# Moving the first weight operands of two stages into the stage ahead, and a token scale behind a DRAM round trip

## The chip, the cores and the metric

The kernel runs on one core of a Trainium2 chip. The metric is device time in microseconds of one execution. Before the change three executions took 1373.17, 1372.91 and 1370.94 us, median 1372.91. Five engines matter here: TensorE (PE, with its weight loads as PEld), VectorE (DVE), ScalarE (ACT), GpSimd (POOL) and SyncE (SP). The last two issue most of the DMAs.

## The reference

One decoder layer on 1024 tokens of width 1024, float32:

```python
h = rmsnorm(x, ln_mix); z = h @ w_in          # q, k, v, g, pool channels pu, gate logits
ret = retention_chunkwise(rotary(q), rotary(k), v)          # 4 heads, chunks of 128
y_ret = (silu(g) * groupnorm(ret) * gn_gain) @ w_ret_up
y_pool = multiscale_pool(pu, pool_w, pool_scale) @ w_pool_up   # windows 2, 4, 8, 16
mixed = sigmoid(gate_A) * y_ret + sigmoid(gate_B) * y_pool
x = x + mixed @ w_o
x = x + relu(rmsnorm(x) @ w_up) ** 2 @ w_down
out = rmsnorm(x, ln_final)
```

The pooling is linear in its input: moving sums over 2, 4, 8 or 16 tokens, divided by the count, minus the token itself.

## The kernel before

**Numbers.** Each float32 operand is carried as a pair: a rounded high part (ScalarE, line 134 or 94) and the remainder (VectorE, line 135 or 95). A product is three matmuls (high by high, high by low, low by high), `PASSES`. RMSNorm's gain goes into the operand, and the token's scale (`R1` for the first norm, `R2` for the second) is multiplied onto the product when it leaves PSUM.

**Stages.** Projection of q, k, v with the retention of four heads (`rotary`, `values`, `retain`, `transposed`); pooling input (`pool_input`, lines 497 to 505), interleaved with `mixed_blocks`; twelve mixer units for g and the gate logits (`mixer_unit`, lines 535 to 590); retention up-projection with the pooling (`pool`, lines 598 to 620); pooling up-projection; output projection (lines 691 to 718); sixteen up units (`up`, lines 721 to 749); the down projection as four sweeps; the final norm.

**The seven-product units.** Mixer and up units (`seven`, lines 180 to 245) multiply a 2 by 2 arrangement of blocks with seven block products in place of eight, in the form with shared sums (T1 to T4 on the token side, s1 to s4 on the weight side). A unit loads 1 MB of weights (line 182), forms s3, s1, s2 and s4 on VectorE (line 192), splits seven stationary operands (lines 134 and 135), and multiplies each with four moving blocks, 12 matmuls of 128x512 for each product, into PSUM banks X, Y, Z and V. The moving blocks of T1 to T4 are sums over tokens' halves: `mixed_blocks(k)` makes block k for the mixer (load from DRAM at line 509, scale at 512, sums at 520, splits), and `moving_operands` (lines 672 to 689) makes block k for up.

**First units.** With `late` (mixer 0 and up 0), the unit first does three quarters of four products:

```python
        if late:
            rest = (3,)
            for x, (ps, made) in groups.items():
                stationary(x, *made)
                mult(ps, x, range(3))
```

so the fourth moving block may come last. All of it stands in program order behind the whole stage ahead: for mixer 0 behind `mixed_blocks(3)` and the transposes of head 3's result (`transposed`, lines 463 to 473); for up 0 behind the copies of R2 (line 718), whose sums need the last residual add (line 706).

**Order of the work.** The engines' instruction streams are not in the order of the text: the tile framework schedules them at build time over a simulated time line, earlier text first where two instructions are ready. Each engine then runs its own stream in order. Buffers rotate: four of tag `w` (8 KB in each partition: weight pieces, raw unit weights, units' temporaries, `xw` blocks), nine of tag `a` (stationary operands of the units, `u`, `rn`, `retn`, `m`, `x1`, `R1`, `R2`), sixteen each of `h` and `r`, five PSUM banks `mm` and three `aux`. A tile waits until the tile that held its buffer is done with.

**Around the change.** `pool_input(g)` multiplies 48 times 128x512, and VectorE takes each half out of PSUM times R1 (line 504) into `u`, which goes to DRAM (line 505). `pool(g)` reads it back some 250 us later (line 601). In the output projection's last block row (k = 3) the order is tile 3 then tile 7 for the first half of the tokens, then both for the second.

Of the kernel before, what the change touches and what calls it, by code (L numbers as in the profile page):

```python
# [16 lines left out]
P = 128  # L17
# [21 lines left out]
def block_kernel(ctx: ExitStack, tc: tile.TileContext, a: dict, out: bass.AP):  # L39
# [33 lines left out]
    def pair_tile(tag, name):  # L73
        return a_tile(tag, name, F32R, (P, 2, HALF))
# [7 lines left out]
    def w_tile(name, dtype=F32R):  # L82
        return wpool.tile([P, 2 * S], dtype, tag="w", name=name)
# [93 lines left out]

    B11, B21, B22, T1, T2, T3, T4 = range(7)

    def seven(name, src, moving, done, late=False, after=None):  # L180
        raw = w_tile(f"raw_{name}", F32)
        nc.sync.dma_start(raw, src)
        raw = raw.rearrange("p (b j) -> p b j", b=4)
        a11, a12, a22, a21 = (raw[:, i, :] for i in range(4))
        tmp = w_tile(f"tmp_{name}", F32).rearrange("p (b j) -> p b j", b=4)
        p1, u2, u4, s3 = (tmp[:, i, :] for i in range(4))
        s1, s2, s4 = a21, a11, a12
        ws = {}

        def stationary(x, src, *adds):  # L190
            for dst, u, v in adds:
                nc.vector.tensor_tensor(dst, u, v, ALU.add)  # L192
            ws[x] = pair_tile("a", f"w{x}_{name}")
            split_pair(ws[x], src)

        def mult(ps, x, ks=range(4), start=True):
            for k in ks:
                for n, (sa, sb) in enumerate(PASSES):
                    nc.tensor.matmul(  # L199
                        ps, ws[x][:, sa, k * P : (k + 1) * P], moving[x][k][:, sb, :],  # L200
                        start=start and k == 0 and n == 0, stop=k == 3 and n == 2,
                        skip_group_check=not start,
                    )

        X, Y = mm_bank(f"ps_X{name}"), aux_bank(f"ps_Y{name}")
        Z, V = mm_bank(f"ps_Z{name}"), mm_bank(f"ps_V{name}")
        groups = {
            B11: (X, (a11,)),
            T2: (Y, (s2, (s3, a11, a21), (s1, a21, a22), (s2, s1, a11))),
            T1: (Z, (s1,)),  # L210
            T3: (V, (s3,)),
        }
        rest = range(4)
        if late:
            rest = (3,)
            for x, (ps, made) in groups.items():
                stationary(x, *made)
                mult(ps, x, range(3))

        def opening(x):  # L220
            ps, made = groups[x]
            if not late:
                stationary(x, *made)
            mult(ps, x, rest)

        def closing(ps, x, *made):
            stationary(x, *made)
            mult(ps, x, start=False)

        opening(B11)  # L230
        nc.scalar.activation(p1, X, AF.Copy)
        opening(T2)
        nc.vector.tensor_tensor(u2, p1, Y, ALU.subtract)
        closing(X, B21, a12)
        done(0, 0, X)
        if after:
            after()
        opening(T1)
        nc.vector.tensor_tensor(u4, u2, Z, ALU.add)
        opening(T3)  # L240
        done(1, 1, V, u4)
        closing(Z, B22, s4, (s4, a12, s2))
        done(0, 1, Z, u2)
        closing(V, T4, a22)
        done(1, 0, V, u2)

    def token_blocks(lo, hi):
# [249 lines left out]
    def pool_input(g):  # L497
        w = load_piece(a["w_fm"][8 + g], f"w_pu{g}")
        u = a_tile("a", f"u{g}")
        for half in range(2):  # L500
            sl = slice(half * HALF, (half + 1) * HALF)
            ps = mm_bank(f"ps_pu{g}_{half}")
            feature_major(ps, w, hT, half)
            nc.vector.tensor_tensor(u[:, sl], ps, R1[:, sl], ALU.mult)
        nc.gpsimd.dma_start(u_dram[g], u)

    def mixed_blocks(k):
# [17 lines left out]
    for g in range(1, 4):  # L525
        pool_input(g)
        mixed_blocks(g - 1)
    mixed_blocks(3)
    transposed(NH - 1, rn)

# [1 line left out]
    ret_dram = dram_tile("ret_dram", (KT // 2, P, 2, S))  # L532
    sg_dram = dram_tile("sg_dram", (2 * KT, P, S))

    def mixer_unit(i, late=False, after=None):
        swish = i < 4
        f0 = i if swish else (i - 4) // 4 * KT + i % 4
        tiles = (f0, f0 + 4)
        o = [a_tile("h", f"mx{i}_{f}") for f in tiles]
        if swish:  # L540
            for m, f in enumerate(tiles):
                nc.gpsimd.dma_start(o[m], retn_dram[f])
        left = [2, 2]

        def done(m, half, ps, add=None):
            sl = slice(half * HALF, (half + 1) * HALF)
            dst, f = o[m][:, sl], tiles[m]
            sign = -1.0 if m else 1.0
            if swish:
                t = rpool.tile([P, 2, HALF], F32, tag="raw", name=f"sw{f}_{half}")  # L550
                z, sig = t[:, 0, :], t[:, 1, :]
            else:
                z = ps if add is None else dst
            y = ps
            if add is not None:
                nc.vector.tensor_tensor(z, add, ps, ALU.add)
                y = z
            if swish:
                nc.vector.scalar_tensor_tensor(z, y, sign, R1[:, sl], ALU.mult, ALU.mult)
                nc.scalar.activation(sig, z, AF.Sigmoid)  # L560
                nc.vector.scalar_tensor_tensor(
                    dst, dst, vec[:, V_GNG + f : V_GNG + f + 1], sig, ALU.mult, ALU.mult
                )
                nc.vector.tensor_tensor(dst, dst, z, ALU.mult)
            else:
                nc.vector.tensor_tensor(z, y, R1[:, sl], ALU.mult)
                nc.scalar.activation(
                    dst, z, AF.Sigmoid, scale=sign, bias=vec[:, V_BG + f : V_BG + f + 1]
                )
            left[m] -= 1  # L570
            if not left[m]:
                nc.gpsimd.dma_start(ret_dram[f // 2, :, f % 2, :] if swish else sg_dram[f], o[m])

        seven(f"mx{i}", a["w_mix"][i], hx, done, late=late, after=after)

    retT = []

# [9 lines left out]
                    retT[-1].append(dst)  # L587

    for i in range(12):
        mixer_unit(i, late=i == 0, after=load_ret if i == 11 else None)  # L590


    pw_raw, pw = a_tile("r", "pw_raw", shape=(P, HALF)), pair_tile("r", "pw")
# [4 lines left out]
    def pool(g):  # L598
        win = WINDOWS[g]
        u = a_tile("r", f"uf{g}")  # L600
        nc.sync.dma_start(u, u_dram[g])
        cur = u
        step = 1
        while step < win:
            nx = a_tile("r", f"s{g}_{step}")
            nc.vector.tensor_copy(nx[:, :step], cur[:, :step])
            nc.vector.tensor_tensor(nx[:, step:], cur[:, step:], cur[:, : S - step], ALU.add)
            cur = nx
            step *= 2
        nc.vector.tensor_tensor(cur[:, :16], cur[:, :16], corr[:, g, :], ALU.mult)  # L610
        nc.vector.scalar_tensor_tensor(cur, cur, 1.0 / win, u, ALU.mult, ALU.subtract)
        ypT.append([])
        for half in range(2):
            pooled = pair_tile("r", f"pooled{g}_{half}")
            split_pair(pooled, cur[:, half * HALF : (half + 1) * HALF])
            ps = aux_bank(f"ps_pw{g}_{half}")
            exact(ps, lambda s: pw[:, s, g * P : (g + 1) * P], lambda s: pooled[:, s, :])
            dst = pair_tile("h", f"ypT{g}_{half}")
            split_scaled(dst, ps, vec[:, V_PSC + g : V_PSC + g + 1])
            ypT[g].append(dst)  # L620
# [70 lines left out]
    for k in range(4):  # L691
# [2 lines left out]
        if k == 3:  # L694
            order = [(f, half) for half in range(2) for f in (k, k + 4)]
        ws = {}
        for f, half in order:
            if f not in ws:
                x1[f] = a_tile("a", f"x1_{f}")
                nc.gpsimd.dma_start(x1[f], a["xT"][f * P : (f + 1) * P, :])  # L700
                ws[f] = load_piece(a["w_o"][f], f"w_o{f}")
                gained[f] = a_tile("r", f"gained{f}")
            sl = slice(half * HALF, (half + 1) * HALF)
            ps = mm_bank(f"ps_o{f}_{half}")
            feature_major(ps, ws[f], mixT, half)
            nc.vector.tensor_tensor(x1[f][:, sl], x1[f][:, sl], ps, ALU.add)
            add_squares(sums2[:, half, :], x1[f][:, sl], f == 0, f"{f}_{half}")
            nc.scalar.activation(
                gained[f][:, sl], x1[f][:, sl], AF.Copy,
                scale=vec[:, V_LNL + f : V_LNL + f + 1],  # L710
            )
# [1 line left out]
            nc.gpsimd.dma_start(x1_dram[f], x1[f])  # L713
        moving_operands(h2, k, gained[k], gained[k + 4], "r" if k < 2 else "h")
    R2 = a_tile("a", "R2")
    for half in range(2):
        sl = slice(half * HALF, (half + 1) * HALF)
        nc.vector.tensor_copy(R2[:, sl], token_rstd([sums2[:, half, :]], f"b{half}"))


    def up(j):
# [8 lines left out]
        def done(m, half, ps, add=None):  # L730
# [13 lines left out]
                nc.gpsimd.dma_start(act_dram[3][j], t4)  # L744

        seven(
            f"up{j}", a["w_up"][j], h2, done, late=j == 0,
            after=begin_down if j == NJ - 1 else None,
        )


# [329 lines left out]
```

## Time and profile before

| | us |
|---|---|
| median of three executions | 1372.91 |
| lowest, highest | 1370.94, 1373.17 |
| profiled execution, its own time | 1370.83 |
| its span, first to last instruction | 1369.0 |
| TensorE busy (6572 matmuls) | 1353.6 |
| VectorE busy | 987.9 |
| ScalarE busy | 565.1 |
| GpSimd busy | 86.1 |
| mean granted TensorE clock | 0.997 |

Times in rows are microseconds from the span's start. A row of a timeline gives start, duration, engine, line, operation, what it writes and reads, and a count where like instructions follow each other; in brackets stands the idle time of that engine just before, and what ended it. Matmuls overlap, so the duration of a row of matmuls ends later than the next row starts. A row of the windows gives the stretch and its length, each engine's busy time in it with the count of instructions, then the granted TensorE clock as a share of 2.4 GHz, the busy share of the DMA engines, and GB/s.

### The profile page before, as it was taken

What the parts mean: (1) busy time and instruction counts of PE and PEld (TensorE: products, weight loads), DVE (VectorE), ACT (ScalarE), POOL (GpSimd) and SP (SyncE); (2) the same over time, 40 slices, a digit from 0 to 9 for tenths busy, and PEclk for the clock granted to TensorE, in tenths of its full rate; (3) what the DMA queues carried; (4) which work ended last, traced back from release to release, by engine and by line L of the source; (5) the groups of instructions that cost most, each with busy time, mean ns of one, the idle gap of its engine ahead of it and who ended that gap; (6) DMA issues with size and microseconds to landing.
All of it is one profiled execution on the core that took longest, in us unless ns stands there. A gap on an engine that the chain in (4) does not pass through costs nothing. (4 is left out here: it accounts for less than half of the span.)

```text
span 1369.0 us, 17491 instructions
## 1 busy us (share of the span) xinstructions
PE 1353.6 (99%) x6572; PEld 1138.6 (83%) x6572; DVE 987.9 (72%) x1631; ACT 565.1 (41%) x960; POOL 86.1 (6%) x151
## 2 busy tenths in 40 slices
PE   9999999999999999999999999999999999999997
PEld 6998999878888888888887888888888888888886
DVE  5766565789966768628657878777787977689665
ACT  6234425463334344113445433333333544444372
POOL 0000001111000000000001011101111000000000
PEclk9999999999999999999999999999999999999999
DMA  9122021354342367124422344433437989778423
GB/s 360 50 62 77 17 92 63 124 215 158 121 172 85 112 238 261 62 77 170 154 77 77 116 169 169 151 126 147 169 139 292 407 330 351 261 266 307 159 70 123
DMA packets 65444, 225.07 MB, mean 164 GB/s; under 512 B 7376, under 2 KB 9424, under 8 KB 61264
## 3 DMA queue, kind: packets, MB, share of 16 engines
q1 hardware_dynamic: 47152, 158.66, 32.7%
q0 software_dynamic: 17920, 65.02, 12.5%
q8 instruction: 51, 0.84, 0.3%
q10 hardware_dynamic: 288, 0.29, 0.1%
q14 instruction: 33, 0.27, 0.1%
HBM read 167.31 MB, written 56.62 MB: 164 GB/s over the span
## 5 line engine op out<-in xcount | busy, mean ns | idle before, releaser
L121 PE MATMUL ps_v<-w_v_hi,hT 128*128 128x256 f32 x512 | 96.0, 284 | 0.0
L199 PE MATMUL ps_Xup<-mv,w_up 128*128 128x512 f32 x384 | 93.0, 390 | 1.7 <-DVE w_up L135 1.7
L199 PE MATMUL ps_Zup<-mv,w_up 128*128 128x512 f32 x384 | 92.5, 389 | 0.8 <-ACT w_up L134 0.8
L853 PE MATMUL ps_dnX<-db,da 128*128 128x512 f32 x384 | 93.1, 389 | 0.1
L134 ACT ACTIVATE w_up<-raw_up 128x512 fp32r<-128x512 f32 x96 | 58.3, 627 | 84.4 <-DVE raw_up L192 46.3
L199 PE MATMUL ps_Vup<-mv,w_up 128*128 128x512 f32 x384 | 92.6, 389 | 0.0
L121 PE MATMUL ps_yr<-retT,w_ret 128*128 128x512 f32 x384 | 88.5, 389 | 0.5 <-ACT w_ret L94 0.5
L121 PE MATMUL ps_o<-mixT,w_o 128*128 128x512 f32 x384 | 87.5, 389 | 0.0
L199 PEld LDWEIGHTS ps_Xup<-mv,w_up 128*128 128x128 f32 x384 | 71.9, 188 | 16.9 <-DVE w_up L135 2.1
L121 PEld LDWEIGHTS ps_yr<-retT,w_ret 128*128 128x128 f32 x384 | 72.0, 188 | 15.8 <-ACT w_ret L94 0.9
L199 PEld LDWEIGHTS ps_Zup<-mv,w_up 128*128 128x128 f32 x384 | 72.0, 188 | 15.7 <-ACT w_up L134 0.8
L853 PEld LDWEIGHTS ps_dnX<-db,da 128*128 128x128 f32 x384 | 72.0, 188 | 15.5 <-DVE db L135 0.5
L199 PEld LDWEIGHTS ps_Vup<-mv,w_up 128*128 128x128 f32 x384 | 72.0, 188 | 15.1 <-ACT w_up L134 0.2
L121 PEld LDWEIGHTS ps_o<-mixT,w_o 128*128 128x128 f32 x384 | 72.0, 188 | 15.0
L135 DVE TENSOR_TENSOR w_up<-raw_up,w_up 128x512 fp32r<-128x512 f32 x96 | 64.2, 685 | 26.4 <-ACT w_up L134 26.1
L121 PEld LDWEIGHTS ps_v<-w_v_hi,hT 128*128 128x128 f32 x512 | 80.8, 192 | 0.0
L134 ACT ACTIVATE w_mx<-raw_mx 128x512 fp32r<-128x512 f32 x72 | 43.6, 626 | 86.0 <-DVE raw_mx L192 44.0
L121 PE MATMUL ps_v<-w_v_lo,hT 128*128 128x256 f32 x256 | 72.6, 284 | 0.0
L199 PE MATMUL ps_Xmx<-hT,w_mx 128*128 128x512 f32 x288 | 72.0, 396 | 0.3 <-ACT w_mx L134 0.3
L199 PE MATMUL ps_Vmx<-hx,w_mx 128*128 128x512 f32 x288 | 69.5, 389 | 0.0
L728 ACT ACTIVATE act<-act 128x512 f32<-128x512 f32 x64 | 40.3, 629 | 65.6 <-DVE act L727 62.2
L199 PEld LDWEIGHTS ps_Xmx<-hT,w_mx 128*128 128x128 f32 x288 | 55.1, 192 | 12.5 <-ACT w_mx L134 0.6
(249 smaller groups left out, 2819.9 us busy)
## 6 DMA issues: line engine op xcount, KB each, us to landing
act_dram<-act POOLq DMA_DIRECT2D x48, 512.0 KB, 4.7
ad<-act_dram SPq DMA_DIRECT2D x48, 512.0 KB, 6.6
raw_up<-in_w_up_dram SPq DMA_DIRECT2D x16, 1024.0 KB, 5.0
raw_mx<-in_w_mix_dram SPq DMA_DIRECT2D x12, 1024.0 KB, 6.2
sg_dram<-mx POOLq DMA_DIRECT2D x16, 512.0 KB, 4.7
wa_lo<-in_w_down_dram SPq DMA_DIRECT2D x16, 512.0 KB, 9.0
wb_hi<-in_w_down_dram SPq DMA_DIRECT2D x16, 512.0 KB, 7.5
wc_lo<-in_w_down_dram SPq DMA_DIRECT2D x16, 512.0 KB, 4.3
```

What stands on the lines that cost most here:

```text
L121: nc.tensor.matmul(ps, stationary(k, sa), moving(k, sb), start=i == 0, stop=i == n - 1)
L134: nc.scalar.activation(dst[:, 0, :], src, AF.Copy)
L135: nc.vector.tensor_tensor(dst[:, 1, :], src, dst[:, 0, :].bitcast(F32), ALU.subtract)
L199: nc.tensor.matmul(ps, ws[x][:, sa, k * P : (k + 1) * P], moving[x][k][:, sb, :], start=start and k == 0 and n == 0, stop=k == 3 and n == ...
L728: nc.scalar.activation(dst, dst, AF.Square)
L853: nc.tensor.matmul(banks[i][:, c0 : c0 + n], w[:, sa, i * P : (i + 1) * P], x[:, sb, c0 : c0 + n], start=start and j == 0 and m == 0, stop ...
```

## The change

Three edits. The unit becomes an object: its load, buffers and stationary operands can be begun before its products. Mixer 0's unit is created, and its B11 operand made, ahead of `mixed_blocks(3)`; up 0's unit is created, and B11, T2, T1 and T3 made, ahead of tile 7's first half in the output projection. The token scales R2 move behind up 0's four three-quarter groups. And `pool_input` leaves PSUM by a ScalarE copy without R1, which `pool` multiplies onto the tile that it has read back.

```diff
-    def seven(name, src, moving, done, late=False, after=None):
+    class Unit:
+        def __init__(self, name, src):
+            self.name, self.ws = name, {}
+            raw = w_tile(f"raw_{name}", F32)
+            nc.sync.dma_start(raw, src)
...
+            self.made = {
+                B11: (a11,),
+                T2: (s2, (s3, a11, a21), (s1, a21, a22), (s2, s1, a11)),
+                T1: (s1,), T3: (s3,), B21: (a12,), B22: (s4, (s4, a12, s2)), T4: (a22,),
+            }
+        def stationary(self, x):
+            if x not in self.ws:
+                src, *adds = self.made[x]
+                for dst, u, v in adds:
+                    nc.vector.tensor_tensor(dst, u, v, ALU.add)
+                self.ws[x] = pair_tile("a", f"w{x}_{self.name}")
+                split_pair(self.ws[x], src)
+            return self.ws[x]
+        def begin(self, *xs):
+            for x in xs:
+                self.stationary(x)
+            return self
+    def seven(unit, moving, done, late=False, opened=None, after=None):
...
         if late:
             rest = (3,)
-            for x, (ps, made) in groups.items():
-                stationary(x, *made)
+            for x, ps in groups.items():
                 mult(ps, x, range(3))
+        if opened:
+            opened()
...
@@ pool_input
-            nc.vector.tensor_tensor(u[:, sl], ps, R1[:, sl], ALU.mult)
+            nc.scalar.activation(u[:, sl], ps, AF.Copy)
@@ after pool_input(3) and mixed_blocks(2)
+    first_mx = Unit("mx0", a["w_mix"][0]).begin(B11)
     mixed_blocks(3)
     transposed(NH - 1, rn)
@@ pool
         nc.sync.dma_start(u, u_dram[g])
+        nc.vector.tensor_tensor(u, u, R1, ALU.mult)
@@ output projection
-        for f, half in order:
+        for n, (f, half) in enumerate(order):
+            if k == 3 and n == 1:
+                first_up = Unit("up0", a["w_up"][0]).begin(B11, T2, T1, T3)
@@ token scales, now called by up 0's unit as `opened`
-    for half in range(2):
-        sl = slice(half * HALF, (half + 1) * HALF)
-        nc.vector.tensor_copy(R2[:, sl], token_rstd([sums2[:, half, :]], f"b{half}"))
+    def token_scales():
+        for half in range(2):
+            sl = slice(half * HALF, (half + 1) * HALF)
+            nc.vector.tensor_copy(R2[:, sl], token_rstd([sums2[:, half, :]], f"b{half}"))
```

## Rows read from the trace of the kernel before

**Rows 1.** The page, busy time of the engines and its share of the span.

```profile
PE 1353.6 (99%) x6572; PEld 1138.6 (83%) x6572; DVE 987.9 (72%) x1631; ACT 565.1 (41%) x960; POOL 86.1 (6%) x151
```

**Rows 2.** The chain of work that ended last, up stage: start, us, what.

```profile
816.28 2.72 PE ps_Xup L199 x12
```

**Rows 3.** Windows: stretch, length, PE, PEld, DVE, ACT, POOL busy, clock, DMA, GB/s.

```profile
264.50:281.00 16.50, 16.46 (x72) 13.58 (x73) 15.66 (x39) 10.00 (x16) 7.25 (x10) 1.00 0.93 328
281.00:285.07 4.07, 2.79 (x17) 1.69 (x15) 3.29 (x7) 4.07 (x10) 0.54 (x1) 1.00 0.98 359
285.07:289.78 4.71, 4.71 (x12) 3.47 (x13) 2.57 (x4) 3.62 (x7) 1.06 (x2) 0.64 0.99 400
...
740.30:749.20 8.90, 6.39 (x34) 4.75 (x33) 8.52 (x15) 5.54 (x11) 2.00 (x2) 1.00 0.16 62
...
708.00:724.00 16.00, 16.00 (x73) 13.23 (x72) 5.33 (x8) 3.41 (x7) 0.97 (x2) 1.00 0.36 128
```

**Rows 4.** Timeline of TensorE, pooling input to mixer 0.

```profile
264.54 16.62 PE L121 MATMUL ps_pu<-hT,w_pu 128*128 128x512 f32 x72 [0.22 <-DVE u L504]
281.00 1.91 PE L469 MATMUL ps_rt<-ident,rn 128*128 128x128 f32 x11
...
285.07 4.87 PE L199 MATMUL ps_Xmx<-hT,w_mx 128*128 128x512 f32 x12 [0.34 <-ACT w_mx L134]
289.78 0.62 PE L199 MATMUL ps_Ymx<-hx,w_mx 128*128 128x512 f32 x2
```

**Rows 5.** Timeline of TensorE, output projection to up 0.

```profile
734.74 5.75 PE L121 MATMUL ps_o<-mixT,w_o 128*128 128x512 f32 x24
740.32 0.60 PE L156 MATMUL spread_b<-ident,rstd_b 128*128 128x128 f32 x4
740.68 0.72 PE L199 MATMUL ps_Xup<-mv,w_up 128*128 128x512 f32 x2
743.06 2.55 PE L199 MATMUL ps_Xup<-mv,w_up 128*128 128x512 f32 x10 [1.67 <-DVE w_up L135]
...
747.15 0.73 PE L199 MATMUL ps_Zup<-mv,w_up 128*128 128x512 f32 x2 [0.75 <-ACT w_up L134]
...
748.89 2.33 PE L199 MATMUL ps_Yup<-mv,w_up 128*128 128x512 f32 x9
```

**Rows 6.** Timeline of ScalarE, output projection: tile 7's weights, up 0's first split.

```profile
696.05 1.06 ACT L94 ACTIVATE w_o<-raw_w_o 128x1024 fp32r<-128x1024 f32 x1 [0.83 <-PE ps_o L121]
...
738.66 0.62 ACT L134 ACTIVATE w_up<-raw_up 128x512 fp32r<-128x512 f32 x1
```

**Rows 7.** Timeline of ScalarE, pooling input to mixer 0.

```profile
263.40 1.55 ACT L442 ACTIVATE rn<-ps_ret 128x512 f32<-128x512 f32 x3
...
274.81 2.19 ACT L512 ACTIVATE xw<-xw,vec 128x1024 f32<-128x1024 f32 x2 [1.63 <-DMA xw<-in_xT_dram]
...
280.96 2.06 ACT L456 ACTIVATE rn<-rn,nb,rs 128x256 f32<-128x256 f32 x4
...
284.40 0.61 ACT L134 ACTIVATE w_mx<-raw_mx 128x512 fp32r<-128x512 f32 x1
```

**Rows 8.** Timeline of VectorE, pooling input to mixer 0.

```profile
263.81 3.07 DVE L504 TENSOR_TENSOR u<-ps_pu,R 128x512 f32<-128x512 f32 x5
...
285.66 0.68 DVE L135 TENSOR_TENSOR hx<-xw,hx 128x512 fp32r<-128x512 f32 x1
```

**Rows 9.** Timeline of the issuing queues: last mixed block's load, mixer 0's load.

```profile
268.38 0.71 POOL L509 DMA_DIRECT2D xw<-in_xT_dram  x1 [1.25 <-DVE hx L135]
...
270.31 0.33 SPq L182 DMA_DIRECT2D raw_mx<-in_w_mix_dram  x1
```

**Rows 10.** The tile raw_mx: issue to landing of its twelve loads.

```profile
DMA to landing us min/median/max: 4.9/6.2/8.7
```

**Rows 11.** Tiles uf and ps_pw: ns min/median/max, first and last start us.

```profile
L611 DVE SCALAR_TENSOR_TENSOR s<-s,uf x4: 1216/1226/1228, 534.1 to 566.6; 128x1024 f32<-128x1024 f32 x4
...
L366 PE MATMUL ps_pw<-pooled,pw x24: 389/389/389, 540.4 to 608.6; 128*128 128x512 f32 x24
```

More of the change, by code (lines that the diff above doesn't have):

```diff
@@ L178, in block_kernel @@
     B11, B21, B22, T1, T2, T3, T4 = range(7)
-    def seven(name, src, moving, done, late=False, after=None):
[L181 to L194, printed above, removed]
+    class Unit:
[3 more added lines that the diff above has]
+            nc.sync.dma_start(raw, src)
+            raw = raw.rearrange("p (b j) -> p b j", b=4)
+            a11, a12, a22, a21 = (raw[:, i, :] for i in range(4))
+            tmp = w_tile(f"tmp_{name}", F32).rearrange("p (b j) -> p b j", b=4)
+            self.p1, self.u2, self.u4, s3 = (tmp[:, i, :] for i in range(4))
+            s1, s2, s4 = a21, a11, a12
+            self.made = {
[16 more added lines that the diff above has]
+    def seven(unit, moving, done, late=False, opened=None, after=None):
+        name, p1, u2, u4 = unit.name, unit.p1, unit.u2, unit.u4
         def mult(ps, x, ks=range(4), start=True):
+            w = unit.stationary(x)
             for k in ks:
@@ L199, in mult @@
                     nc.tensor.matmul(
-                        ps, ws[x][:, sa, k * P : (k + 1) * P], moving[x][k][:, sb, :],
+                        ps, w[:, sa, k * P : (k + 1) * P], moving[x][k][:, sb, :],
                         start=start and k == 0 and n == 0, stop=k == 3 and n == 2,
@@ L206, in seven @@
         Z, V = mm_bank(f"ps_Z{name}"), mm_bank(f"ps_V{name}")
[L207 to L212, printed above, removed]
+        groups = {B11: X, T2: Y, T1: Z, T3: V}
         rest = range(4)
@@ L215, in seven @@
             rest = (3,)
-            for x, (ps, made) in groups.items():
-                stationary(x, *made)
+            for x, ps in groups.items():
                 mult(ps, x, range(3))
[L220 to L230, printed above, removed]
+        if opened:
+            opened()
+        mult(X, B11, rest)
         nc.scalar.activation(p1, X, AF.Copy)
-        opening(T2)
+        mult(Y, T2, rest)
         nc.vector.tensor_tensor(u2, p1, Y, ALU.subtract)
-        closing(X, B21, a12)
+        mult(X, B21, start=False)
         done(0, 0, X)
@@ L237, in seven @@
             after()
-        opening(T1)
+        mult(Z, T1, rest)
         nc.vector.tensor_tensor(u4, u2, Z, ALU.add)
-        opening(T3)
+        mult(V, T3, rest)
         done(1, 1, V, u4)
-        closing(Z, B22, s4, (s4, a12, s2))
+        mult(Z, B22, start=False)
         done(0, 1, Z, u2)
-        closing(V, T4, a22)
+        mult(V, T4, start=False)
         done(1, 0, V, u2)
@@ L533, in block_kernel, with mixer_unit @@
     sg_dram = dram_tile("sg_dram", (2 * KT, P, S))
-    def mixer_unit(i, late=False, after=None):
+    def mixer_unit(i, first=None, after=None):
         swish = i < 4
@@ L572, in done @@
                 nc.gpsimd.dma_start(ret_dram[f // 2, :, f % 2, :] if swish else sg_dram[f], o[m])
-        seven(f"mx{i}", a["w_mix"][i], hx, done, late=late, after=after)
+        seven(first or Unit(f"mx{i}", a["w_mix"][i]), hx, done, late=bool(first), after=after)
     retT = []
@@ L589, in block_kernel @@
     for i in range(12):
-        mixer_unit(i, late=i == 0, after=load_ret if i == 11 else None)
+        mixer_unit(i, first_mx if i == 0 else None, load_ret if i == 11 else None)
     pw_raw, pw = a_tile("r", "pw_raw", shape=(P, HALF)), pair_tile("r", "pw")
@@ L746, in up @@
         seven(
-            f"up{j}", a["w_up"][j], h2, done, late=j == 0,
-            after=begin_down if j == NJ - 1 else None,
+            Unit(f"up{j}", a["w_up"][j]) if j else first_up, h2, done, late=j == 0,
+            opened=None if j else token_scales, after=begin_down if j == NJ - 1 else None,
         )
```

## The prediction, made before the changed kernel was built or run

> **What bounds the kernel now.** I read the page's busy times first, then the stages' windows, then TensorE's timeline at the two places the diff touches, and only then the other engines there. TensorE is busy 1353.6 us of a 1369.0 us span [rows 1], so a change that adds or removes no matmul can gain only where TensorE's stream has holes. Busy time overstates how full it is, since consecutive matmuls overlap; the true price is the step from start to start, 2.72 us for 12 matmuls, 0.2267 us each [rows 2]. So I compare starts with what lies between them.
>
> First boundary, pooling input to mixer [rows 3, 4]: from the first transpose of head 3's result at 281.00 to the first Y matmul at 289.78 are 8.78 us. In them lie 16 transposes, at 0.09 us each (four spread transposes start at 740.32 and the next matmul at 740.68 [rows 5]) 1.44 us, and 12 X matmuls, 2.72 us: 4.16. The excess is 4.6 us. Two us of it are speed, not waiting: the 12 X matmuls take 4.71 us from 285.07, at a mean granted clock of 0.64, so mostly at 1.2 GHz; just before, TensorE had been busy 2.79 of 4.07 us. The other 2.6 us are waits: 0.34 for the first weight split, the rest around transposes that wait for ScalarE. A further 0.2 us is lost at 264.54, waiting for a PSUM bank that a pooling eviction holds.
>
> Second boundary, output projection to up [rows 3, 5]: from 740.32 to the first Y at 748.89 are 8.57 us. In them are 8 transposes and 8 ones-matmuls (1.44 us, all at the transposes' price, an estimate) and 16 matmuls of 512 columns (3.63): 5.07. The excess is 3.5 us, of which 1.67 is one wait for the B11 low half on VectorE and 0.75 one for T1 on ScalarE. The clock stays at 1.00 here. **Ceiling: 0.2 + 4.6 + 3.5 = 8.3 us**, 0.6% of the time; no other TensorE wait is touched.
>
> **The change, part by part.** *Second boundary.* Before, B11's high split runs on ScalarE at 738.66 [rows 6], and X's matmuls then wait until 743.06 for its low half on VectorE [rows 5]. It is moved ahead of tile 7's first half, with T2, T1 and T3: 4 ScalarE splits, 4 VectorE splits, 3 additions, one 1 MB load. The projection's order there is tile 3, tile 7 for the first half of the tokens, then both for the second, 24 matmuls or 5.44 us each, the last from 734.74 [rows 5]: so tile 7 starts near 724 and tile 6 ends near 718. VectorE's part is 7 x 0.68 = 4.8 us (0.68 as in [rows 8]); in 708 to 724 it is idle 10.7 of 16 us, ScalarE 12.6 [rows 3]. So the cost is nothing there, and VectorE has some 3 us less to do where it is full, 8.52 of 8.9 us [rows 3]. Moving the token scales behind the four three-quarter groups takes two copies out of VectorE's way; TensorE has 36 matmuls x 0.2267 = 8.2 us in hand while they form. Late next are the fourth blocks of T2 and T3, which need the last residual add, from 740.3 on, and some eight VectorE steps behind it: ready at about 740.3 + 9 x 0.68 = 746.4, wanted at 740.3 + 8.2 + 0.7 (X's last three) = 749.2. B21's weights follow on the same full VectorE. I leave 0.7 us for these (bounds 0, since 749 is met, and 1.7, the longest wait of now; nearer the first) and take 3.5 - 0.7 = **2.8 gained**.
>
> The loan it takes is a weight buffer: four rotate, and unit 0's two come before tile 7's weights. Those move from the buffer that they take at 696.05 [rows 6] to one free when tile 6's matmuls end, near 718; a ScalarE split of 1.06 us [rows 6] and a VectorE split of twice 0.68 fit before 724. Cost 0, and up to 2 us if either is queued behind something.
>
> *First boundary, the eviction.* Eight VectorE multiplications out of PSUM become ScalarE copies; three like copies took 1.55 us [rows 7], some 0.52 each, 4.1 us in all. Around there VectorE is the full engine, 15.66 of 16.5 us, with ScalarE at 10.00 [rows 3]. Five of the multiplications run in a row from 263.81 for 3.07 us [rows 8], 0.61 each, just ahead of the statistics from which head 3's normalization, from 280.96 the last thing that the transposes wait for [rows 7], is made. Taken away, that chain can end up to 3 us sooner, which is more than the 2.3 us lost around the transposes. Bounds 0 (ScalarE becomes the late one: it is busy all 4.07 us from 281.00 to 285.07 [rows 3]) and 2.3; I take 1.6, nearer the upper end since VectorE is the fuller one. Against it: the first copies now stand behind the three evictions from 263.40 [rows 7], so the bank wait of 0.2 us may grow by up to 1.1; I take 0.3.
>
> The Trainium skill, page "ScalarE: Activation LUTs", section "Rules for kernel authors", advises VectorE and not ScalarE for such simple work, and its budget gives an estimate of 0.3 + 512 x 0.83 ns = 0.72 us for each copy, 5.8 us in all. The rows say the opposite for these PSUM reads (0.52 against 0.61); by the page's price the holes would be used up and my 1.6 would go to nearly 0.
>
> *First boundary, the weights.* Mixer 0's load and B11 split move ahead of the last mixed block. Before, the split starts at 284.40 [rows 7], though its data was asked for at 270.31 [rows 9]; a load of this tensor lands in 4.9 to 8.7 us [rows 10]. Split before 281, X follows the projection at once: the 0.34 us wait goes, and with TensorE kept busy the 2.0 us of half clock, 2.3 together. T2's operand (3 additions, one split each on two engines) is wanted 9 x 0.2267 = 2.0 us after X and competes with the last mixed block: 0 to 1.7 us (the like wait of B11 at the second boundary), I take 0.6. First boundary: 2.3 + 1.6 - 0.3 - 0.6 = **3.0 gained**.
>
> *The later token scale.* Four VectorE multiplications of 1024 columns, about 1.2 us each by the last step of pooling. That step starts last at 566.6, and the matmul that uses its tile comes last at 608.6 [rows 11]: hidden by 40 us. R1's buffer is held longer, until pooling ends; the output projection's loads wait for it or another at worst, tens of us before use. Cost 0; without that cover 1.2 us each.
>
> Sum: 2.8 + 3.0 = 5.8. From the profiled execution's 1370.83 that is 1365.0; the median of the three runs stands 2.1 above that execution, so **1367.1**.
>
> **Rivals.**
> A, slower: the buffer ring delays the last mixed block. Its load is issued at 268.38, just before mixer 0's at 270.31 [rows 9]. Mixer 0's two tiles now come first in the ring, so it may get its buffer only when the third block's is done, near 279. Scaled from 274.81 [rows 7], its last operand is ready at 286.34 [rows 8], 11.5 us later. With a load of 6 us from 279 that is 285 to 296.5, and TensorE wants T2 of it at about 281 + 8.2 + 0.7 = 290. It decides from an issue later than some 273. At its worst TensorE idles 6.5 us and pays the 2 us of half clock, 8.5 against 4.6 now: 3.9 lost. If the same ring takes the second boundary's gain, by tile 7's weights (its 3.5 us stay), that is 1376.8; with the 2.8 gained there 1374.0. For it: the DMA engines are 0.93 busy in this stretch [rows 3]. Against: the third block may finish by 276, with VectorE relieved.
> The Trainium skill, "DMA: Bandwidth & Descriptors", section "Issuing engines are not separate DMA queues", has loads of different issuing engines share the same 16 engines; by that rule the earlier weight load would slow the block's load too, which the DMA share and the 8.7 us above bear out.
> B, the first boundary stays: the transposes still wait for the normalization chain, and the clock drops. Gain 2.8 + 0.3: 1369.8.
> C, nothing: the operands that were late are replaced by T2's, B21's and the fourth blocks' on engines as full as before: 1372.9.
> D, all holes close: 1372.9 - 8.3 = 1364.6.
>
> **Chances.** Forecast 0.45, D 0.13, B 0.20, C 0.12, A 0.10. What a measurement here can tell from no change is 0.2%, 2.7 us. Faster: nearly all of the forecast, D, and half of B, 0.67; slower: A, 0.10; the same: the rest, 0.23. The range 1363.6 to 1372.6 takes in D with a margin for the spread of runs (2.2 us in three) and B, and leaves out A and half of C.
>
> **What would show it.** Right: the 12 X matmuls of mixer 0 at 2.7 us, directly after the last pooling matmul or transpose, clock 1.00; no wait of X or Z for the first up unit's splits; those splits before 723; no idle time of TensorE over 1 us from 281 to 292 and from 740 to 760. Wrong: the last mixed block's load issued after 276 and TensorE waiting on its split (A); transposes still waiting on the normalization with half clock behind them (B); a like wait under another name (C); TensorE waiting on the eviction copies for over 1 us, or on tile 7's weights near 723.

## The result, and the profile after

The changed kernel takes **1364.89 us** (median of six executions, 1364.29 to 1365.59) against 1372.75 for the kernel before in the same comparison (six, 1370.28 to 1373.17): 0.9947 of the time, 95% interval 0.9934 to 0.9960. In a later set, with 21 executions of the kernel before, it was 1365.19 against 1371.55: 0.9955 (0.9941 to 0.9969). So 6 to 8 us are gained, where 5.8 were forecast, and the time lies 2.2 us under the predicted 1367.1. The profiled execution took 1365.59 us, 5.2 less than the profiled execution before; its span is 1363.5 us.

The page, busy times of the engines after, to be read beside [rows 1]:

```profile
PE 1350.9 (99%) x6572; PEld 1137.6 (83%) x6572; DVE 988.8 (73%) x1627; ACT 569.0 (42%) x968; POOL 85.6 (6%) x151
```

No engine's total tells the gain: the matmuls are the same 6572, VectorE has not less to do in sum (the eight multiplications return as four of twice the length in the pooling), and ScalarE has 4 us more.

Timeline of TensorE after, first boundary, which answers to [rows 4]:

```profile
265.77 16.64 PE L121 MATMUL ps_pu<-hT,w_pu 128*128 128x512 f32 x72 [0.69 <-ACT u L509]
282.25 1.47 PE L474 MATMUL ps_rt<-ident,rn 128*128 128x128 f32 x12
283.48 3.01 PE L219 MATMUL ps_Xmx<-hT,w_mx 128*128 128x512 f32 x12
286.33 0.60 PE L474 MATMUL ps_rt<-ident,rn 128*128 128x128 f32 x4
286.68 0.70 PE L219 MATMUL ps_Ymx<-hx,w_mx 128*128 128x512 f32 x2
```

From the first transpose to the first Y matmul are now 4.43 us in place of 8.78; the work alone was put at 4.16. No row but the first has a wait, and that wait grew from 0.22 to 0.69 us. Windows of the same stretches (columns as in [rows 3]):

```profile
265.70:282.25 16.55, 16.48 (x72) 13.58 (x73) 11.59 (x32) 14.26 (x26) 6.60 (x10) 1.00 0.97 335
282.25:286.33 4.08, 4.08 (x26) 3.52 (x24) 3.81 (x7) 4.08 (x10) 1.08 (x2) 1.00 0.98 335
```

In the first line VectorE went from 15.66 to 11.59 us and ScalarE from 10.00 to 14.26 [rows 3]: the two have changed places. The granted clock stays at 1.00, where 4.71 us at 0.64 stood before.

ScalarE's timeline after, answering to [rows 7]:

```profile
264.17 1.06 ACT L447 ACTIVATE rn<-ps_ret 128x512 f32<-128x512 f32 x2
265.12 2.55 ACT L509 ACTIVATE u<-ps_pu 128x512 f32<-128x512 f32 x5
...
274.73 2.07 ACT L461 ACTIVATE rn<-rn,nb,rs 128x256 f32<-128x256 f32 x4
...
278.22 0.62 ACT L134 ACTIVATE w_mx<-raw_mx 128x512 fp32r<-128x512 f32 x1
280.15 2.19 ACT L517 ACTIVATE xw<-xw,vec 128x1024 f32<-128x1024 f32 x2 [1.30 <-DMA xw<-in_xT_dram]
```

The second group of four normalizations starts at 274.73, not 280.96; the B11 split at 278.22, not 284.40; the five copies stand behind the two evictions of the line above.

Timeline of TensorE after, second boundary, answering to [rows 5]:

```profile
709.39 1.92 PE L219 MATMUL ps_Yup<-mv,w_up 128*128 128x512 f32 x6
...
740.01 0.60 PE L156 MATMUL spread_b<-ident,rstd_b 128*128 128x128 f32 x4
740.37 2.33 PE L219 MATMUL ps_Xup<-mv,w_up 128*128 128x512 f32 x9
742.54 2.20 PE L219 MATMUL ps_Zup<-mv,w_up 128*128 128x512 f32 x9
...
746.62 0.84 PE L219 MATMUL ps_Xup<-mv,w_up 128*128 128x512 f32 x3
```

Both waits, 1.67 and 0.75 us, are gone. Nine Y matmuls have moved into the output projection, six of them at 709.39: 1.76 us from start to start for what takes 1.36 at 0.2267 each.

To compare many kernels I count one thing in each profiled execution: the time from a matmul's start to the next one's, less what the step takes undisturbed (0.227, 0.120 and 0.110 us for 512, 256 and fewer columns), where it is over 0.04 us. "Bank" is the step into the last quarter of the pooling input, "first" and "second" the boundaries (to 306 and 700 to 760 us), "read-back" 505 to 526 us, where the retention result comes back from DRAM. The kernels are those of the next section, where eviction, mixer and up are called E, M and U.

| us lost by TensorE | bank | first | read-back | second | median time |
|---|---|---|---|---|---|
| before | 0.49 | 4.29 | 0.76 | 3.59 | 1372.75 |
| the whole change | 0.95 | 0.18 | 0.77 | 1.02 | 1364.89 |
| only_eviction | 0.95 | 1.50 | 0.77 | 3.58 | 1369.09 |
| only_mixer | 0.49 | 7.00 | 0.77 | 3.58 | 1373.01 |
| only_up | 0.49 | 3.66 | 0.77 | 1.30 | 1369.36 |
| no_eviction | 0.49 | 4.79 | 0.77 | 1.12 | 1369.18 |
| no_mixer | 0.95 | 1.43 | 0.77 | 1.07 | 1366.41 |
| no_up | 0.95 | 0.18 | 0.76 | 3.58 | 1367.99 |
| before_again | 0.49 | 5.14 | 0.76 | 3.59 | 1371.66 |
| unit_earlier | 0.95 | 1.73 | 5.79 | 0.88 | 1369.83 |
| after_again | 0.95 | 0.18 | 0.76 | 1.07 | 1365.19 |
| first_copy_vector | 0.49 | 0.18 | 0.77 | 1.26 | 1364.48 |
| only_mixer_all | 0.49 | 3.60 | 4.69 | 3.58 | 1374.29 |
| no_eviction_all | 0.49 | 3.61 | 4.54 | 0.98 | 1371.77 |

The change wins 4.11 at the first boundary and 2.57 at the second and loses 0.46 at the bank: 6.2. The start of the kernel, its first 14 us with the waits for the first tiles, cost 4.4 to 5.4 us by the same count in these executions, whatever the kernel, and happened to cost 0.75 more in the profiled execution after: that leaves 5.5, the difference of the spans.

### The profile page after: what moved, and what is told of

It reads as the page before. It is cut to its first block, busy times and chain, and to the rows that moved or that the text cites. A ratio compares the mean times of both kernels' runs of the same rounds, so it can differ in the third digit from the quotient of the medians.

```text
span 1363.5 us, 17493 instructions
## 1 busy us (share of the span) xinstructions
PE 1350.9 (99%) x6572; PEld 1137.6 (83%) x6572; DVE 988.8 (73%) x1627; ACT 569.0 (42%) x968; POOL 85.6 (6%) x151
## 4 chain that ended last, share of the span: by engine, by line
PE 93%; DMA 2%; issue 2%; ACT 1%; DVE 1%; POOL 0%; SPq 0%; POOLq 0%; DVEq 0%; ACTq 0%
PE ps_v L121 7%; PE ps_o L121 6%; PE ps_yr L121 6%; PE ps_dnZ L864 6%; PE ps_Xup L219 6%; PE ps_dnX L864 6%; PE ps_Zup L219 6%; PE ps_dnV L864 6%; PE ps_Vup L219 6%; PE ps_Xmx L219 5%; PE ps_Zmx L219 4%; PE ps_Vmx L219 4%; PE ps_kT L121 3%; PE ps_yp L121 3%; PE ps_pu L121 3%; PE ps_qT L121 3%
## 5 line engine op out<-in xcount | busy, mean ns | idle before, releaser
L219 PEld LDWEIGHTS ps_Vmx<-hx,w_mx 128*128 128x128 f32 x288 | 54.1, 188 | 11.2
```

The lines of the kernel that those rows point to most:

```text
L219: nc.tensor.matmul(ps, w[:, sa, k * P : (k + 1) * P], moving[x][k][:, sb, :], start=start and k == 0 and n == 0, stop=k == 3 and n == 2, s ...
```

## The experiments

Three sets, each with its own executions of the kernel before beside it, medians 1371.69 (31 of them), 1371.92 (26) and 1371.55 (21). E is the eviction with the later token scale, M the first mixer unit's B11 split ahead, U the first up unit's four splits ahead and the later token scales. The unit as an object is in all. The whole change itself was timed in the comparison above and in the third set, so where a kernel of the first two sets is compared with it, both of its medians are used; the medians of the kernel before agree within 0.4 us between the sets.

**E alone.**

```diff
-            nc.vector.tensor_tensor(u[:, sl], ps, R1[:, sl], ALU.mult)
+            nc.scalar.activation(u[:, sl], ps, AF.Copy)
...
+        nc.vector.tensor_tensor(u, u, R1, ALU.mult)
```

> Only the pooling input's eviction on ScalarE with the scale applied in pooling; both first units as before. Two theories of the first boundary. Chain theory: VectorE, relieved of the eight multiplications, ends head 3's normalization some 6 us sooner (its last group on ScalarE near 275 instead of 281), the 2.3 us around the transposes go, but X still waits for the B11 split that stands behind them; 1.5 to 3 us faster than before, the clock at full or half in the X matmuls. Filler theory: the gain comes from having X ready as work for TensorE while the transposes wait; then the eviction alone gives under 0.5 us, less the longer wait for the bank (0.5 us), so within 1 us of before.

Measured: 1369.09 (1368.48 to 1369.45), ratio 0.9979 (0.9969 to 0.9988). That is 2.6 us faster, as the chain theory had it; the filler theory gave under 1 us. Timelines of this kernel, ScalarE's lines, then TensorE's:

```profile
274.28 2.18 ACT L517 ACTIVATE xw<-xw,vec 128x1024 f32<-128x1024 f32 x2
...
277.40 2.07 ACT L461 ACTIVATE rn<-rn,nb,rs 128x256 f32<-128x256 f32 x4
```

```profile
282.19 2.04 PE L474 MATMUL ps_rt<-ident,rn 128*128 128x128 f32 x16
285.05 3.29 PE L219 MATMUL ps_Xmx<-hT,w_mx 128*128 128x512 f32 x12 [0.82 <-ACT w_mx L134]
```

The second normalization comes 3.6 us sooner than before [rows 7] (6 were expected), the 16 transposes run in one piece, and the X matmuls run at full clock although a wait of 0.82 us for B11 stands just ahead of them. That moving the evictions clears the transposes is shown. The path is another than the one expected, through VectorE's statistics. VectorE's lines of the kernel before: the two splits behind the evictions, and the last step of the statistics for the second normalization.

```profile
266.80 1.28 DVE L135 TENSOR_TENSOR hx<-xw,hx 128x512 fp32r<-128x512 f32 x2
...
278.00 0.15 DVE L454 SCALAR_TENSOR_TENSOR nb<-mv,rs 128x4 f32<-128x4 f32 x1
```

The statistics were ready at 278.15, and the normalization that uses them started only at 280.96 [rows 7]. In between ScalarE had no pause: from 274.81 it worked on the last mixed block, for whose load it had stood idle 1.63 us, and then on the normalizations. U alone (below), where the first boundary is untouched, has the same order and a later load; its lines on ScalarE:

```profile
275.82 2.20 ACT L517 ACTIVATE xw<-xw,vec 128x1024 f32<-128x1024 f32 x2 [2.87 <-DMA xw<-in_xT_dram]
...
281.97 2.06 ACT L461 ACTIVATE rn<-rn,nb,rs 128x256 f32<-128x256 f32 x4
```

The load landed 1.0 us later and the normalization started 1.0 us later, 6.15 us behind the block's scaling in both; so it is in the second profile of the kernel before (275.71 and 281.86). The transposes waited for that load, which stood ahead of the normalizations in ScalarE's queue. The evictions stood ahead of the load in turn: the two splits follow them on VectorE, and the issue at 268.38 waited for such a split [rows 9]. With E alone GpSimd issues it 2.3 us sooner:

```profile
266.12 0.71 POOL L514 DMA_DIRECT2D xw<-in_xT_dram  x1 [1.68 <-DVE hx L135]
```

ScalarE then no longer waits for it, and the order of its queue has the first normalization ahead of the block, not behind it. How much of the 3.6 us comes from the sooner load and how much from the order was not separated.

**M alone.**

```diff
+    first_mx = Unit("mx0", a["w_mix"][0]).begin(B11)
     mixed_blocks(3)
```

> Only mixer 0's load and B11 split ahead of the last mixed block; eviction on VectorE and up 0 as before. Chain theory: the transposes still wait for the normalization near 283, TensorE's order has them ahead of X or X fills only part; 0 to 1.5 us faster than before, half clock still seen. Filler theory: X's 12 matmuls run between the transposes, no half clock; 3 to 4.5 us faster than before.

Measured: 1373.01 (1370.85 to 1373.64), ratio 1.0003 (0.9994 to 1.0012): nothing gained, the lower end of the chain theory. Timelines of this kernel, TensorE's lines, then ScalarE's and VectorE's:

```profile
287.15 0.73 PE L219 MATMUL ps_Ymx<-hx,w_mx 128*128 128x512 f32 x2 [1.60 <-ACT w_mx L134]
...
291.75 4.07 PE L219 MATMUL ps_Ymx<-hx,w_mx 128*128 128x512 f32 x10 [2.83 <-DVE w_mx L135]
```

```profile
286.47 1.14 ACT L134 ACTIVATE w_mx<-raw_mx 128x512 fp32r<-128x512 f32 x2
```

```profile
290.40 0.69 DVE L202 TENSOR_TENSOR tmp_mx<-raw_mx 128x512 f32<-128x512 f32 x1 [3.58 <-DMA raw_mx<-in_w_mix_dram]
291.01 1.29 DVE L135 TENSOR_TENSOR w_mx<-raw_mx,w_mx 128x512 fp32r<-128x512 f32 x2
```

X does follow the projection at once, and fills the time in which the transposes were awaited. But T2's operand is late on both engines. Its high half stands in ScalarE's queue until 286.47, behind the last block's splits and a copy of the transposes: the hole of 1.60 us. Its low half stands on VectorE behind an addition for the *second* mixer unit, which waits 3.58 us for that unit's load: the hole of 2.83 us. (In the kernel before that addition came at 289.95, after T2's low half at 287.64.) The ten Y matmuls behind the second hole take 3.91 us from start to start, against 2.48 for ten, nearly all at full clock, in the kernel of all but E (291.48 to 293.96): 1.4 us of half clock.

**U alone.**

```diff
+            if k == 3 and n == 1:
+                first_up = Unit("up0", a["w_up"][0]).begin(B11, T2, T1, T3)
```

> Only up 0's operands ahead of tile 7 and the token scales behind the four groups; the first boundary as before. Both theories: the waits of 1.67 and 0.75 us are gone, 2.5 to 3.5 us faster than before, with the first boundary's half clock unchanged (X of mixer 0 at 4.7 us for 12). If the boundaries are not independent, the gain differs from this by over 1 us.

Measured: 1369.36 (1367.88 to 1371.77), ratio 0.9980 (0.9972 to 0.9989). That is 2.3 us faster, just under the 2.5 expected at the least. The second boundary's loss falls from 3.59 to 1.30, of which 0.83 stand at the hoisted Y matmuls. The half clock expected at the first boundary did not come in the profiled execution: its 12 X matmuls take 3.13 us from start to start.

**All but E, all but M, all but U.** The same edits, one taken back at a time.

> The whole change but for the eviction, which stays on VectorE with its scale. Chain theory: loses 2 to 4 us of the change's 7.9 against before, so 4 to 6 us faster than before. Filler theory: loses nothing and even gets back the 0.5 us of the bank wait, 7.5 to 8.5 us faster than before.

> The whole change but for mixer 0's early load and split. Chain theory: only the wait of X for its split stays; 1 to 2.5 us slower than the change (5.5 to 7 us faster than before). Filler theory: the whole first boundary is lost, 4 to 5 us slower than the change.

> The whole change but for up 0: operands and token scales as before. Both theories: 2.5 to 3.5 us slower than the change, that is 4.5 to 5.5 us faster than before; the waits of 1.7 and 0.75 us return by name.

Measured: without E 1369.18 (1367.64 to 1371.75), ratio 0.9980 (0.9972 to 0.9989); without M 1366.41 (1366.03 to 1367.30), 0.9962 (0.9950 to 0.9975); without U 1367.99 (1367.33 to 1370.07), 0.9977 (0.9968 to 0.9986). Against the whole change they lose 4.0 to 4.3, 1.2 to 1.5 and 2.8 to 3.1 us (by either of its medians). Without E the loss is at the upper end of what was expected or just above it, and the kernel is only 2.5 us faster than before, where both theories gave 4 us or more. M and U lose what was expected. Without U the gain over the kernel before is 3.9 us, under the 4.5 expected; these expectations started from the 7.9 us of the first comparison, and the third set gives 6.4. So M is worth nothing alone and 1.2 to 1.5 us beside E: with VectorE relieved, the transposes and B11 are both there in time, and the 0.82 us wait for B11, with the start behind it, is all that M still removes (1.43 against 0.18 in the table). U's gain stands apart from the other two.

**The kernel before once more.**

> The kernel before, unchanged, profiled and timed again. Its six times so far lie in two groups, near 1370.5 and 1372.9 us; the change's six lie within 1.3 us. Theory: the half-clock stretch at the first boundary is longer in some executions (some 2 us lost at 1.2 GHz, or some 4), which shows as a mean granted clock of 0.997 in the shorter runs and 0.995 to 0.996 in the longer ones. Rival: the two groups have the same clock, and the spread is in the loads at the start.

Measured: 1371.66 (1369.86 to 1374.42), ratio 0.9997 (0.9988 to 1.0006). Its profiled execution has the half clock too; its lines on TensorE's timeline, then those of U alone, where TensorE's matmuls up to there are the same, in the same order:

```profile
284.98 0.66 PE L469 MATMUL ps_rt<-ident,rn 128*128 128x128 f32 x4 [0.67 <-ACT retn L472]
285.98 4.77 PE L199 MATMUL ps_Xmx<-hT,w_mx 128*128 128x512 f32 x12 [0.34 <-ACT w_mx L134]
```

```profile
285.08 0.66 PE L474 MATMUL ps_rt<-ident,rn 128*128 128x128 f32 x4 [0.67 <-ACT retn L477]
286.08 3.29 PE L219 MATMUL ps_Xmx<-hT,w_mx 128*128 128x512 f32 x12 [0.34 <-ACT w_mx L134]
```

The same work after the same waits (two more, of 0.68 or 0.69 and 0.16 us, stand ahead of these in both) took 4.77 us in one execution and 3.29 in the other. Windows of the two, in the same order:

```profile
285.00:300.00 15.00, 14.66 (x58) 11.57 (x59) 10.24 (x17) 7.45 (x15) 1.37 (x3) 0.89 0.48 185
```

```profile
285.00:300.00 15.00, 14.58 (x64) 11.68 (x65) 11.65 (x20) 8.82 (x18) 1.48 (x3) 1.00 0.56 220
```

The granted clock is 0.89 in the one and 1.00 in the other: behind the same holes the half clock came in one execution and not in the other. That it lasts longer in the longer executions, as the theory had it, is not shown: in both profiles of the kernel before there is one such stretch at this boundary. They do show a second thing that varies: the last mixed block's load landed 0.9 us later in this profile than in the first, and the last transposes started 0.9 us later.

**The ring, provoked.** The unit begun one mixed block earlier, so that its two tiles also go ahead of the third block's:

```diff
     for g in range(1, 4):
         pool_input(g)
+        if g == 3:
+            first_mx = Unit("mx0", a["w_mix"][0]).begin(B11)
         mixed_blocks(g - 1)
-    first_mx = Unit("mx0", a["w_mix"][0]).begin(B11)
```

> The change with mixer 0's unit one block earlier still, ahead of the third mixed block, so that its buffers come ahead of two blocks' in the ring. The price of the ring, rival A of the prediction: the third and the last block's loads issue later by 3 to 10 us, the last block's operands after 290, and TensorE waits for them: 1 to 6 us slower than the change. If the ring has slack, within 0.7 us of the change.

Measured: 1369.83 (1368.57 to 1371.94), ratio 0.9985 (0.9976 to 0.9994), 4.6 to 4.9 us above the whole change. Its waits on TensorE:

```profile
PE ps_yr L121 <- ACT w_ret L94: 2.7, 1, 2.7
...
PE ps_Ymx L219 <- ACT w_mx L134: 1.3, 1, 1.3
```

The last line is the expected price, in part: the third block's load is issued 2.4 us later than in the whole change (266.11 against 263.75), the last block's no later (271.76 against 271.83). The third block's splits run later on ScalarE, the fourth's after them, and the weights that Y wants behind these, 1.3 us late (the order is read from the queue). The first line was not expected: 230 us on, the read-back of the retention result starts at 498.30 in place of 477.94, and TensorE waits 2.7 us for `w_ret`, whose splits stand behind those of the late tiles, with 2.8 us of half clock after it. In the table the first boundary loses 1.6 us more than in the whole change and the read-back 5.0; so the expected 1 to 6 us were met mainly by something else than the price of the ring at the last blocks. Why a changed order at 265 us shifts the buffers at 480 us was not followed.

**The whole change again, and with one copy back on VectorE.**

```diff
+            if (g, half) == (0, 0):
+                nc.vector.tensor_copy(u[:, sl], ps)
+            else:
                 nc.scalar.activation(u[:, sl], ps, AF.Copy)
```

> The changed kernel once more, beside the three below on one chip. If its runs agree because no stretch at half clock is left in it, they lie at 1364.3 to 1365.6 again, all with a mean clock of 0.998, while those of the kernel before spread over 4 to 5 us, the longer ones at 0.995 to 0.996. If the narrow spread came by chance, some of its runs reach 1367 or more, or a clock under 0.997.

> The changed kernel with the first of the eight copies of the pooling input back on VectorE (a plain copy, unscaled). Theory: the 0.69 us that TensorE stands still at the start of the last quarter is ScalarE's queue, in which that copy stands behind two normalising copies of 1.06 us; then it falls to about 0.2 us, as before the change, and the time by 0.4 to 0.6 us, to about 1364.4. Rival: the bank is late for another reason (a copy takes its time on either engine): the wait stays at 0.6 to 0.7 us and the time at 1364.9.

Measured: 1365.19 (1364.90 to 1365.59) and **1364.48** (1364.24 to 1364.96), ratios 0.9955 (0.9941 to 0.9969) and 0.9949 (0.9937 to 0.9961). TensorE's line of the second kernel:

```profile
265.20 16.62 PE L121 MATMUL ps_pu<-hT,w_pu 128*128 128x512 f32 x72 [0.22 <-DVE u L510]
```

The wait is 0.22 us again: ScalarE's queue it was. The medians differ by 0.7 us, the table's losses by 0.3; the executions of the two nearly part, but both figures are below what the comparison with the kernel before resolves. Its median is the lowest of the kernels run here. The whole change's spread was again narrow, 0.7 us, and its times within those expected; but one of five executions had a mean clock of 0.996, under 0.997, which had been named as a sign of chance. It took 1365.59 us, 0.4 above the median.

**All four first operands ahead, without E.** `begin(B11, T2, T1, T3)` for the mixer's first unit too, alone and together with U.

> The kernel before with the first mixer unit's weights moved, but all four first operands split in the stage ahead, not B11 alone; copies of the pooling input stay on VectorE. Theory: B11 alone won nothing because VectorE's queue then held an addition for the next unit's weights, which waited for their load until 290.3 us, ahead of the low halves of the other three operands. With those three split ahead of it, no wait of Ymx for w_mx is left, and of the 4 us of holes at this boundary 2 to 4 go: 1368 to 1370. Rival: VectorE is too full without the copies moved to ScalarE, whatever the order: the holes move to the last block's operands (Ymx or Zmx waits for hx, or the transposes wait for rn) and the time stays at 1371 to 1373.

> The same four operands ahead, with the up unit's move as well: the whole change but the copies on ScalarE. Theory: if the four operands ahead close the first boundary without the copies moved, this stands at about 1365 to 1366, level with the whole change, and ScalarE's longer wait at the bank is saved. Rival: VectorE is too full: 1368 to 1370, where the change without the copies moved stood (1369.2).

Measured: 1374.29 (1373.78 to 1375.07), ratio 1.0021 (1.0012 to 1.0030), slower; and 1371.77 (1370.65 to 1372.70), 0.9996 (0.9988 to 1.0005). Both lie above what either theory gave, by 1.3 and 1.8 us at the least. The holes of M alone are indeed gone from 287 to 292 us: in the first of the two kernels TensorE's timeline has no wait between 264.88 and 297.77. Then come other lines, GpSimd's queue first, then TensorE's:

```profile
281.31 0.71 POOL L514 DMA_DIRECT2D xw<-in_xT_dram  x1 [1.66 <-DVE nb L459]
```

```profile
297.77 0.50 PE L219 MATMUL ps_Xmx<-hT,w_mx 128*128 128x512 f32 x1 [0.82 <-DVE w_mx L135]
```

The last mixed block's load is issued at 281.31, not 268.38 [rows 9], and lands at 290.94. Its four parts are made beside weight operands, and those then come late: 0.82 us here and a wait of Y for 1.46 us at 302.70. That is the late load of rival A, with the issue later than the 273 named there; but TensorE waits for weights that share the two queues with the block, not for the block. The second loss is at the read-back again (4.69 and 4.54 in the table). So the holes of M alone came from T2's late operand, and curing them that way costs more than the holes. Whether VectorE's queue alone made them is not separated, since the edit moves the splits on both engines.

## Why the prediction was right, and where it was not

**The ceiling and the place** held. The 8.3 us counted in holes are what these places lose in the table (0.49, 4.29 and 3.59); 6.2 of them went, and the read-back, the other place in it, kept its loss.

**Second boundary, 2.8 forecast, 2.57 measured.** The splits stand at 699 and 708 to 710 us, and the waits are gone. The table still has 1.02 us there, about the 0.7 left for the fourth blocks and B21, for another reason: no operand is late, but 0.54 us are lost in four steps at the six Y matmuls that the scheduler puts into the projection, and the rest in five steps of 0.09 to 0.10 where TensorE comes back from short matmuls (two such stood there before). The loaned weight buffer cost nothing: ScalarE's split of tile 7's weights, timeline of ScalarE after, against 696.05 in [rows 6]:

```profile
716.80 1.06 ACT L94 ACTIVATE w_o<-raw_w_o 128x1024 fp32r<-128x1024 f32 x1 [3.65 <-PE ps_o L121]
```

It comes where the prediction put it, before 718, and no matmul waits on it.

**First boundary, 3.0 forecast, 3.65 measured (4.11 less 0.46).** The step that failed is the split of this sum between the parts; that the sum came near is in part luck, since the errors have opposite signs. It gave 2.3 us, the B11 wait and the half clock, to the moved weights, and 1.6 to the eviction. The runs give the eviction 2.8 of the 4.1 us at the boundary, the 1.6 us of half clock of that execution among them, and the moved weights 1.3, and those only once the eviction is there: alone they only changed the order in which late operands were late. The half clock was put at 2.0 us, 4.71 less 2.72; at full clock and behind the same wait the 12 X matmuls take 3.13 (U alone, E alone), so 1.6 is the clock and 0.4 the start behind a wait. The path was wrong too: the prediction has the transposes wait for VectorE's statistics, and the rows under E alone have them wait for the last mixed block's load, itself held back by the evictions. Three more terms were mis-sized. The transposes: 1.6 of 2.3 us were taken, "up to 3 us sooner" for the chain; the second normalization starts 3.6 us sooner with E alone and 6.2 in the whole change, and all 2.3 went. The further 2.6 us, as the two queues read, come from the ring: the last block's load, issued 3.5 us later than before and 5.7 later than with E alone, leaves ScalarE free for the normalization where that block's scaling stood with E alone. T2's wait: 0.6 taken, none measured. The bank: 0.3 taken, 0.46 measured, and the experiment with one copy confirms the reason given.

The prediction weighed the price of a ScalarE copy from the Trainium skill, "ScalarE: Activation LUTs", section "Rules for kernel authors": an estimate of 0.72 us, by which little would have come of the eviction. The budget there is for an ACTIVATE with a pointer operand as its bias, and these copies have none. Here five copies took 2.55 us in a row, 0.51 each, and E alone, against the advice to keep such work on VectorE, gained 2.6 us at a place where VectorE was busy 15.66 of 16.5 us and ScalarE 10.00 [rows 3].

**The ring (rival A)** did happen and did not decide. The timeline of GpSimd after, and of the issuing queue SP (two issues in one row, the first at 265.92):

```profile
271.83 0.76 POOL L514 DMA_DIRECT2D xw<-in_xT_dram  x1 [1.32 <-PE ps_pu L121]
```

```profile
265.92 16.85 SPq L186 DMA_DIRECT2D raw_mx<-in_w_mix_dram  x2
```

The block's load moved from 268.38 to 271.83 [rows 9], behind a pooling matmul, and the mixer's from 270.31 to 265.92. That is 1.2 us short of the 273 from which A was said to decide, and TensorE waits for nothing; an issue at 281.31 (all four operands ahead, without E) had waits of 0.82 and 1.46 us behind it, where 6.5 us of idling were A's worst.

**The token scale** cost nothing. Line by tile `uf`, after:

```profile
L608 DVE TENSOR_TENSOR uf<-uf,R x4: 1219/1220/1226, 526.9 to 560.7; 128x1024 f32<-128x1024 f32 x4
```

Four of 1.22 us, as estimated; the last matmul on the pooled tiles starts at 605.6 us and the last pooling step at 569.1, so most of the cover of 40 us is there.

**The median.** 5.8 forecast and 5.24 measured between profiled executions would have given 1365.6. The prediction then added 2.1 us, by which the median before stood above its own profiled execution. That term is wrong: it is no constant of the measurement. After the change the median stands 0.7 *under* the profiled execution. The executions of the kernel before in the three sets show what it was:

| mean granted clock | executions | mean time, us |
|---|---|---|
| 0.995 | 12 | 1373.3 |
| 0.996 | 17 | 1373.1 |
| 0.997 | 42 | 1371.2 |
| 0.998 | 7 | 1369.9 |

On the mean, the longer executions have the lower clock; 0.001 of the clock over 1369 us is 1.4 us, where the steps between rows are 0.2, 1.9 and 1.3. Single executions overlap: at 0.996 they run from 1371.4 to 1375.5, at 0.997 from 1369.3 to 1372.6. So the clock is a part of the spread and not all of it; the landing of the last block's load, 0.9 to 1.0 us apart in the profiles, is another. Of the whole change's eleven executions ten are at 0.998, and all lie within 1.3 us. That a part of the gain in medians is spread taken away with the holes, and that the extra time lies at the first boundary, is argued, not shown: outside the profiled executions only the mean clock is known. In the profiled ones the second boundary ran at full clock before as well.

The median of 1364.89 thus lies beside rival D's 1364.6, in which all holes close, but D did not happen: 2.15 us of loss are left at the three places in the table.

## What to carry to other kernels

When TensorE is 99% busy, count its loss from start to start at each stage's boundary; then ask which engine's queue the late operand stood in and what the work ahead of it there waits for (here a load), because moving one operand ahead only uncovers the next if that engine stays full. Work moved from a full engine to a half-empty one made the early weights worth something here; neither was worth as much alone. And with an order made at build time, each begun tile takes a buffer: look at when the loads behind it are issued, at that place and in later stages.

## What was not expected of the hardware

After the same waits, the last two of 0.67 and 0.34 us, TensorE ran the same 12 matmuls in 4.77 us at a granted clock that averaged 0.89 over 15 us, and in 3.29 us at 1.00: whether the clock falls to 1.2 GHz after holes of that size differs from execution to execution, and the kernel before spreads over 4.4 to 5.8 us in the three sets, where the same work without the holes spreads over 1.3 (eleven executions).
